# Half-array products of the mixers stage written in pairs, and retention taken two heads at a time

## The chip, the cores and the metric

The kernel runs on one core of one Trainium2 chip. The metric is the time of one execution on the device in microseconds; the figure for the kernel before is the median of its runs. TensorE multiplies matrices into PSUM, VectorE (DVE) and ScalarE (ACT) empty PSUM and do the elementwise work, GpSimd (POOL) does some elementwise work out of SBUF, and SyncE (SP) issues the loads of weights.

## The reference, cut to what matters

A first block (dilated attention, stick-breaking attention, two mixtures of experts) is followed by two layers of a second block, on 256 tokens of width 1024. A layer is `x + 0.5 ffn1`, then the mixers, then `+ 0.5 ffn2`. The mixers take `h = rmsnorm(x)`, project it with `w_in`, and run four mixers of width 256 beside each other, each with four heads of 64:

- a short convolution;
- RWKV-7 in both directions: per step `S = S * w + (S @ -kk) (kk * a)^T + v k^T`, `y = S @ r`;
- retention: `o[i] = sum_j (q_i . k_j) * gamma^|i-j| * v_j` for every head, then an RMS norm and a SiLU gate;
- MLA, an attention with low-rank queries and keys.

Their outputs, side by side, go through `w_out` and are added to `x`.

## The kernel before, in words

Everything is fp32. The large projections are split into three fp32r products each (`mm3`, L243 to L247); the small products inside the mixers are plain fp32 (`mm`, L249 and L250), and the trace shows two matmul records for each of those.

`mixers` (L1105) runs once a layer. A tile keeps the features of two heads in its 128 partitions, 64 each. A product that contracts over the 64 features of one head therefore reads partitions 0 to 63 or 64 to 127, and uses the lower or the upper half of the rows of TensorE's array.

RWKV is computed in two chunks of 128 tokens (*stages*) by a chain of small products:

- **NT** (L1501 to L1509): for each group g (0, 1) and each half i (0, 1), four products of 64 x 128 by 128 columns (two directions d, two head pairs hp) into one PSUM buffer psC, and one masked multiply of 128 x 512 on VectorE that empties it into NT.
- **the M chain** (L1532 to L1605): the inverse of each head's triangular matrix, first in squares of 32 rows, with a VectorE step after each set of products, two groups in turn, then the larger blocks with F, H and X.
- **products(stage, d, hp)** (L1514 to L1525): for each half hh one psC buffer, a product of KA with 256 columns and one of BE with 128 columns, and one masked multiply of 128 x 384 on VectorE. It is called four times for stage 0 before the stages (L1611) and once in each of the last four steps of stage 0 for stage 1 (L1661), there behind the copy of a psC buffer to ysum.
- the steps R, U, S and ysum of both stages.

In the trace AR, an input of NT and of `products`, appears as tile x.

The rest of the stage is a generator, `pieces` (L1310): the rotary products, retention, the latents of MLA, the convolution, MLA's attention and the first parts of the output projection, cut into pieces by `yield`. `fill()` (L1487) lets the generator go on by as many pieces as the next digit of `TURNS` (L163) says; it stands behind each step of the chain, so that TensorE has projections and other work while VectorE and ScalarE finish a link.

**Retention** in `pieces`: `head(h)` (L1338) makes two score products (64 rows, 256 columns, keys j = 0, 1, each into a psB buffer), each emptied by a multiply with the decay on VectorE (L1345), then four value products into a third psB buffer, and an eviction into yr (rT in the trace). Heads 0 and 1 are called at the second and the fourth step of the gate's projection (L1357 to L1360), head 2 behind the first latent (L1367), head 3 behind the other latents (L1380).

PSUM: psA has four buffers (projections), psB two, psC two. `evac` (L533) empties PSUM by ScalarE and VectorE in turn. Tiles of one name share their buffers in rotation; a new one waits for the release of the oldest. "t", which holds the scores, has eight. The framework sets each engine's order when it builds the program: among the instructions whose inputs and buffers are ready by its plan, the earliest in the code goes first, and later work may go ahead of earlier work that waits.

Of the kernel before, what the change touches and what calls it, by code (L numbers as in the profile page):

```python
# [11 lines left out]
OP = mybir.AluOpType  # L12
# [157 lines left out]
class Net:  # L170
# [934 lines left out]
    def mixers(self, x, l):  # L1105
        nc, A = self.nc, self.A
        v, act, gp = nc.vector, nc.scalar.activation, nc.gpsimd
        tt, stt, ts = v.tensor_tensor, v.scalar_tensor_tensor, v.tensor_scalar
        with self.tc.tile_pool(name="mix", bufs=1) as sp:
# [4 lines left out]
            def new(name, n=256, dt=F32):  # L1114
                return sp.tile([128, n] if isinstance(n, int) else n, dt, name=name, bufs=bufs.get(name, 1))
# [55 lines left out]
            chs = lambda c: slice(c * 128, c * 128 + 128)  # L1171
# [15 lines left out]
            AR, KA, BE, fac, wa, E = {}, {}, {}, {}, {}, {}  # L1187
# [3 lines left out]
            for h in range(2):  # L1191
                w4 = self.row().rearrange("p (d a t) -> p d a t", d=2, a=2)
                LL = self.row()[:, :516].rearrange("p (d c t) -> p d c t", d=2, c=2)
                for d in range(2):
                    wa[d, h] = w4[:, d]
                    r = slice(64 * d, 64 * d + 64)
                    p = self.psC()
# [8 lines left out]
                    for c in range(2):  # L1206
                        o, i = raw[:, c, inc(d)], wa[d, h][:, 0, chs(c)]
                        if d:
                            o, i = o[:, ::-1], i[:, ::-1]
# [14 lines left out]
            for h in range(2):  # L1224
                p = chunk(2 + h)
# [26 lines left out]
            for h in range(2):  # L1252
                p = self.psC()
# [3 lines left out]
            for d, h in both:  # L1257
                t = new("t")
# [21 lines left out]
            u, out = {}, {}  # L1280
# [29 lines left out]
            def pieces():  # L1310
                p = yield from chunk_parts(21)
# [4 lines left out]
                qk = {}  # L1316
                for n, i in (("q", 7), ("k", 9)):
                    for hp in range(2):
                        q = new("t")
                        p = yield from chunk_parts(i + hp)  # L1320
                        self.evac(q, p[:, :256])
                        p = self.psB()
                        self.mm(p[:, :256], self.r64, q)
                        o, t = new("rq"), new("t")
# [10 lines left out]
                rv, rg, yr = new("kT", [128, 2, 256]), new("kf", [128, 2, 256]), new("rT", [128, 8, 64])  # L1335
                yield from rows(1, lambda c, p: self.evac(rv[:, c, :], p))

                def head(h):  # L1338
                    r = slice(h % 2 * 64, h % 2 * 64 + 64)
                    ST = []  # L1340
                    for j in range(2):
                        p = self.psB()
                        self.mm(p[:, :256], qk["k", h // 2][r, chs(j)], qk["q", h // 2][r, :])
                        st = new("t")
                        tt(out=st, in0=p[:, :256], in1=self.decay[:, h, 128 * (1 - j):128 * (1 - j) + 256], op=OP.mult)  # L1345
                        ST.append(st)
                    p = self.psB()
                    for c in range(2):
                        for j in range(2):
                            self.mm(p[:, c * 64:c * 64 + 64], ST[j][:, chs(c)], rv[:, j, h * 64:h * 64 + 64], j == 0, j == 1)  # L1350
                    self.evac(yr.rearrange("p (c h) d -> p c h d", c=2)[:, :, h, :], p[:, :128].rearrange("p (c d) -> p c d", c=2))

                def silu2(c, p):
                    act(rg[:, c, :], p, AF.Tanh, scale=0.5)
                    stt(out=rg[:, c, :], in0=rg[:, c, :], scalar=1.0, in1=p, op0=OP.add, op1=OP.mult)

                for h, _ in enumerate(rows(2, silu2)):  # L1357
                    if h % 2:
                        head(h // 2)
                    yield  # L1360

                late = new("late", 1664)
# [1 line left out]
                qb = late[:, :1152].rearrange("p (k c) -> p k c", k=3)  # L1364
                kvb = late[:, 1152:]
                (ckv,), rk = yield from latent((11,), 3, "la")
                head(2)  # L1367
                yield
                qa, rq = yield from latent((12, 13, 14), 0, "la")
                ex = new("t")  # L1370
# [1 line left out]
                p = self.psB()  # L1372
# [4 lines left out]
                rqs = new("rqs", 4)  # L1377
                ts(rqs[:, :2], rq, scale, None, op0=OP.mult)
                ts(rqs[:, 2:], rq, -scale, None, op0=OP.mult)
                head(3)  # L1380

                sq = g8(new("kT", [128, 2, 256]))
                act(sq, yr, AF.Square)
# [7 lines left out]
                for i, n in enumerate(("x", "c", "b")):  # L1391
                    for h in range(2):
                        p = yield from chunk_parts(15 + 2 * i + h)
# [3 lines left out]
                        elif n == "c":  # L1397
                            t = new("t", 258)
# [12 lines left out]
                for c in range(2):  # L1411
                    p = self.psB()
# [4 lines left out]
                for j in range(2):  # L1417
                    p = self.psB()
# [6 lines left out]
                for j in range(2):  # L1425
                    p = self.psB()
# [4 lines left out]
                p = self.psB()  # L1431
                for i in range(3):
                    self.mm(p[:, :256], qb[:, i, 256:], qa[i], i == 0, i == 2)
                q = new("t")
# [19 lines left out]
                for h in range(6):  # L1454
                    if h < 4:
                        p = halves(self.psB())
# [9 lines left out]
                    if 1 <= h <= 4:  # L1466
                        i, Q, m = last
                        t, pt = self.psB(), new("X", 512)
# [4 lines left out]
                        for k in range(4):  # L1473
                            self.mm(o[:, k // 2 * 64:k // 2 * 64 + 64], pt[:, chs(k)], mv[:, k % 2, i * 64:i * 64 + 64], k % 2 == 0, k % 2 == 1)
                        tt(out=ym[:, :, i * 64:i * 64 + 64], in0=o[:, :128].rearrange("p (c d) -> p c d", c=2),
                           in1=m[:, 6:8, None].to_broadcast([128, 2, 64]), op=OP.mult)
# [22 lines left out]
            fill()  # L1499
            two = range(2)  # L1500
            for g in two:  # L1501
                for i in two:
                    p = self.psC()
                    for d in two:
                        c = chunk_of(g, d)
                        for hp in two:
                            x0, x1 = AR[d, hp][half(i), c, 0, :], BE[d, hp][half(i), chs(c)]
                            self.mm(p[:, chs(2 * d + hp)], *((x0, x1) if d else (x1, x0)))
                    tt(out=NT[:, 8 * g + i:8 * g + 8:2, :], in0=p.rearrange("p (q t) -> p q t", q=4), in1=self.nmask, op=OP.mult)  # L1509
            fill()  # L1510

# [2 lines left out]
            def products(stage, d, hp):  # L1514

                c = chunk_of(stage, d)
                t = self.row().rearrange("p (h a t) -> p h a t", h=2, a=4)
                for hh in two:
                    ar = AR[d, hp][half(hh), c, :, :]
                    p = self.psC()  # L1520
                    self.mm(p[:, :256], KA[d, hp][half(hh), chs(c)], ar)
                    self.mm(p[:, 256:384], BE[d, hp][half(hh), chs(c)], ar[:, 1, :])
                    tt(out=t[:, hh:hh + 1, :3, :], in0=p[:, :384].rearrange("p (h a t) -> p h a t", h=1, a=3),
                       in1=self.gmask[d], op=OP.mult)
                G[stage, d, hp] = t  # L1525
# [218 lines left out]
```

## Time and profile before

| | us |
|---|---|
| median of 3 runs | 2017.63 |
| lowest, highest run | 2016.68, 2024.1 |
| the profiled execution, its own time | 2027.7 |
| its span | 2025.7 |
| TensorE busy | 1919.8 (95%) |
| VectorE busy | 1186.3 (59%) |
| ScalarE busy | 862.8 (43%) |
| GpSimd busy | 193.3 (10%) |

The span runs from the first to the last instruction; the execution's own time has some 2 us around it. TensorE counts as busy while a matmul is under way, and matmuls overlap, so the time that a group costs is read from its first start to the start of what follows it, not from the length of its records. The mixers of layer 0 lie at about 1039 to 1206 us of the span, those of layer 1 at 1643 to 1815 us.

### The profile page before, as it was taken

To read this page: it belongs to the slowest core of one execution; us is meant where nothing else is said; L and a number is where in the kernel's file an instruction comes from. 1 tells how busy PE (TensorE), PEld (TensorE's weight loads), DVE (VectorE), ACT (ScalarE), POOL (GpSimd) and SP (SyncE) were. 2 spreads that over 40 slices of the span, in tenths; PEclk is the share of its full clock that TensorE was granted. 3 is DMA by queue.
4 is the path that set the end of the run, shared out by engine and by line. 5 is a ranking of instruction groups with operands and counts; after the bars stand their busy time and mean duration, and the time that the engine had idled before them with its cause. 6 is when DMAs were issued, how large, how long until landed. Compare 5 with 4: busy or idle time off the path is not lost. (4 is left out here: it accounts for less than half of the span.)

```text
span 2025.7 us, 36997 instructions
## 1 busy us (share of the span) xinstructions
PE 1919.8 (95%) x14866; PEld 1622.0 (80%) x14866; DVE 1186.3 (59%) x2329; ACT 862.8 (43%) x1786; POOL 193.3 (10%) x225
## 2 busy tenths in 40 slices
PE   7999997997897997999999999999999999999998
PEld 7999996434885443899888988998999888888997
DVE  6778775125876124855576556555555675556554
ACT  5656552112662112544543335445544533235443
POOL 1323220000220000000021100000000030100000
PEclk9999998998998998999998999999999999899999
DMA  8345346795436796655532215555555532215553
GB/s 280 126 137 164 127 135 240 278 408 191 146 125 222 268 388 232 211 188 187 184 113 77 93 62 178 185 188 168 199 187 188 188 103 83 84 61 176 189 186 107
DMA packets 102516, 357.10 MB, mean 176 GB/s; under 512 B 11888, under 2 KB 15136, under 8 KB 102208
## 3 DMA queue, kind: packets, MB, share of 16 engines
q1 hardware_dynamic: 97584, 341.70, 49.1%
q10 hardware_dynamic: 4704, 12.81, 2.0%
q8 instruction: 120, 1.97, 0.4%
q14 instruction: 60, 0.49, 0.1%
q0 software_dynamic: 48, 0.13, 0.0%
HBM read 353.53 MB, written 1.07 MB: 175 GB/s over the span
## 5 line engine op out<-in xcount | busy, mean ns | idle before, releaser
L241 DVE TENSOR_TENSOR wlo<-raw,whi 128x512 fp32r<-128x512 f32 (+1 forms) x910 | 626.1, 715 | 384.0 <-ACT whi L240 380.1
L240 ACT ACTIVATE whi<-raw 128x512 fp32r<-128x512 f32 (+1 forms) x910 | 529.8, 616 | 592.3 <-issue 197.6
L245 PE MATMUL psB<-xTh,whi 128*128 128x256 f32 x1792 | 507.7, 283 | 12.3 <-ACT whi L240 8.3
L247 PE MATMUL psB<-xTh,wlo 128*128 128x256 f32 x1792 | 506.4, 283 | 0.2 <-DVE wlo L241 0.2
L246 PE MATMUL psB<-xTl,whi 128*128 128x256 f32 x1792 | 506.1, 282 | 0.4
L245 PEld LDWEIGHTS psB<-xTh,whi 128*128 128x128 f32 x1792 | 340.1, 190 | 18.1 <-ACT whi L240 9.8
L246 PEld LDWEIGHTS psB<-xTl,whi 128*128 128x128 f32 x1792 | 340.1, 190 | 5.4 <-DVE xTl L241 1.5
L247 PEld LDWEIGHTS psB<-xTh,wlo 128*128 128x128 f32 x1792 | 340.3, 190 | 1.4 <-DVE wlo L241 0.7
L247 PE MATMUL psA<-whi,hl 128*128 128x512 f32 x352 | 139.5, 396 | 0.0
L245 PE MATMUL psA<-whi,hh 128*128 128x512 f32 x352 | 139.4, 398 | 0.0
L246 PE MATMUL psA<-wlo,hh 128*128 128x512 f32 x352 | 138.7, 394 | 0.0
L245 PE MATMUL psA<-xTh,whi 128*128 128x256 f32 (+1 forms) x352 | 107.8, 307 | 0.3 <-ACT vt L536 0.2
L247 PE MATMUL psA<-xTh,wlo 128*128 128x256 f32 (+1 forms) x352 | 105.1, 299 | 0.0
L246 PE MATMUL psA<-xTl,whi 128*128 128x256 f32 (+1 forms) x352 | 103.6, 295 | 0.3 <-DVE xTl L241 0.3
L245 PE MATMUL psB<-whi,xTh 128*128 128x384 f32 (+2 forms) x256 | 90.3, 353 | 3.6 <-DVE qs L547 1.7
L247 PE MATMUL psB<-whi,xTl 128*128 128x384 f32 (+2 forms) x256 | 88.7, 347 | 0.4 <-DVE xTl L241 0.3
L246 PE MATMUL psB<-wlo,xTh 128*128 128x384 f32 (+2 forms) x256 | 88.5, 346 | 0.3 <-DVE wlo L241 0.3
L296 POOL TENSOR_TENSOR ss<-ss,mh 128x1 f32<-128x1 f32 x14 | 9.8, 702 | 785.5 <-DVE ss L295 780.8
L250 PE MATMUL psB<-raw,XT 128*64 128x512 f32 x288 | 83.5, 601 | 0.0
L247 PEld LDWEIGHTS psA<-whi,hl 128*128 128x128 f32 x352 | 66.0, 188 | 16.8 <-DVE hl L241 0.7
L246 PEld LDWEIGHTS psA<-wlo,hh 128*128 128x128 f32 x352 | 66.6, 189 | 12.6
L245 PEld LDWEIGHTS psA<-whi,hh 128*128 128x128 f32 x352 | 66.3, 188 | 12.8 <-ACT hh L240 0.9
(414 smaller groups left out, 3036.1 us busy)
## 6 DMA issues: line engine op xcount, KB each, us to landing
raw<-in_ffn1gu_dram SPq DMA_DIRECT2D x88, 512.0 KB, 3.8
raw<-in_ffn2gu_dram SPq DMA_DIRECT2D x88, 512.0 KB, 3.7
raw<-in_egu_dram SPq DMA_DIRECT2D x72, 512.0 KB, 9.9
wf<-in_egu_dram SPq DMA_DIRECT2D x56, 512.0 KB, 8.6
raw<-in_dqk_dram SPq DMA_DIRECT2D x46, 512.0 KB, 3.9
raw<-in_ffn1dn_dram SPq DMA_DIRECT2D x44, 512.0 KB, 3.6
raw<-in_ffn2dn_dram SPq DMA_DIRECT2D x44, 512.0 KB, 3.6
raw<-in_wb_dram SPq DMA_DIRECT2D x40, 512.0 KB, 3.7
```

The costliest lines, as they stand in the source:

```text
L240: self.hi = self.nc.scalar.activation(hi, src, AF.Copy)
L241: return (self.nc.gpsimd if pool else self.nc.vector).tensor_tensor(out=lo, in0=src, in1=hi.bitcast(F32), op=OP.subtract)
L245: mm(out, a[0], b[0], start=start, stop=False)
L246: mm(out, a[0], b[1], start=False, stop=False)
L247: mm(out, a[1], b[0], start=False, stop=stop)
L250: return self.nc.tensor.matmul(out, a, b, start=start, stop=stop)
L296: nc.gpsimd.tensor_tensor(out=ss[:, 3:4], in0=ss[:, 2:3], in1=self.mh[:, :1], op=OP.pow)
```

## The change

Three places in `mixers`:

- NT: both psC buffers of a group are taken first, and the products of the two halves alternate; then both buffers are emptied.
- `products`: both psC buffers are taken first, then KA of both halves, BE of both halves, and both multiplies.
- Retention: `heads(hp)` takes two heads. For each j it takes two psB buffers, makes the score of both heads (one on each half of the rows), and empties both; the eight value products of both heads go into one psB buffer, emptied by one eviction. `heads(0)` stands where head 0 stood, `heads(1)` where head 2 stood; the calls for heads 1 and 3 are gone from their places.

The numbers of products and of multiplies stay as they are; `TURNS` is not changed.

```diff
--- before.py
+++ after.py
@@ -1335,28 +1335,32 @@
                 rv, rg, yr = new("kT", [128, 2, 256]), new("kf", [128, 2, 256]), new("rT", [128, 8, 64])
                 yield from rows(1, lambda c, p: self.evac(rv[:, c, :], p))
 
-                def head(h):
-                    r = slice(h % 2 * 64, h % 2 * 64 + 64)
-                    ST = []
+                def heads(hp):
+
+                    ST = {}
                     for j in range(2):
-                        p = self.psB()
-                        self.mm(p[:, :256], qk["k", h // 2][r, chs(j)], qk["q", h // 2][r, :])
-                        st = new("t")
-                        tt(out=st, in0=p[:, :256], in1=self.decay[:, h, 128 * (1 - j):128 * (1 - j) + 256], op=OP.mult)
-                        ST.append(st)
-                    p = self.psB()
-                    for c in range(2):
-                        for j in range(2):
-                            self.mm(p[:, c * 64:c * 64 + 64], ST[j][:, chs(c)], rv[:, j, h * 64:h * 64 + 64], j == 0, j == 1)
-                    self.evac(yr.rearrange("p (c h) d -> p c h d", c=2)[:, :, h, :], p[:, :128].rearrange("p (c d) -> p c d", c=2))
+                        ps = [self.psB() for _ in range(2)]
+                        for i in range(2):
+                            r = slice(i * 64, i * 64 + 64)
+                            self.mm(ps[i][:, :256], qk["k", hp][r, chs(j)], qk["q", hp][r, :])
+                        for i, p in enumerate(ps):
+                            st = ST[i, j] = new("t")
+                            tt(out=st, in0=p[:, :256], in1=self.decay[:, 2 * hp + i, 128 * (1 - j):128 * (1 - j) + 256], op=OP.mult)
+                    p = self.psB()[:, :256].rearrange("p (c h d) -> p c h d", c=2, h=2)
+                    for i in range(2):
+                        h = 2 * hp + i
+                        for c in range(2):
+                            for j in range(2):
+                                self.mm(p[:, c, i, :], ST[i, j][:, chs(c)], rv[:, j, h * 64:h * 64 + 64], j == 0, j == 1)
+                    self.evac(yr.rearrange("p (c h) d -> p c h d", c=2)[:, :, 2 * hp:2 * hp + 2, :], p)
 
                 def silu2(c, p):
                     act(rg[:, c, :], p, AF.Tanh, scale=0.5)
                     stt(out=rg[:, c, :], in0=rg[:, c, :], scalar=1.0, in1=p, op0=OP.add, op1=OP.mult)
 
                 for h, _ in enumerate(rows(2, silu2)):
-                    if h % 2:
-                        head(h // 2)
+                    if h == 1:
+                        heads(0)
                     yield
 
                 late = new("late", 1664)
@@ -1364,7 +1368,7 @@
                 qb = late[:, :1152].rearrange("p (k c) -> p k c", k=3)
                 kvb = late[:, 1152:]
                 (ckv,), rk = yield from latent((11,), 3, "la")
-                head(2)
+                heads(1)
                 yield
                 qa, rq = yield from latent((12, 13, 14), 0, "la")
                 ex = new("t")
@@ -1377,7 +1381,6 @@
                 rqs = new("rqs", 4)
                 ts(rqs[:, :2], rq, scale, None, op0=OP.mult)
                 ts(rqs[:, 2:], rq, -scale, None, op0=OP.mult)
-                head(3)
 
                 sq = g8(new("kT", [128, 2, 256]))
                 act(sq, yr, AF.Square)
@@ -1499,13 +1502,14 @@
             fill()
             two = range(2)
             for g in two:
-                for i in two:
-                    p = self.psC()
-                    for d in two:
-                        c = chunk_of(g, d)
-                        for hp in two:
+                ps = [self.psC() for _ in two]
+                for d in two:
+                    c = chunk_of(g, d)
+                    for hp in two:
+                        for i in two:
                             x0, x1 = AR[d, hp][half(i), c, 0, :], BE[d, hp][half(i), chs(c)]
-                            self.mm(p[:, chs(2 * d + hp)], *((x0, x1) if d else (x1, x0)))
+                            self.mm(ps[i][:, chs(2 * d + hp)], *((x0, x1) if d else (x1, x0)))
+                for i, p in enumerate(ps):
                     tt(out=NT[:, 8 * g + i:8 * g + 8:2, :], in0=p.rearrange("p (q t) -> p q t", q=4), in1=self.nmask, op=OP.mult)
             fill()
 
@@ -1515,11 +1519,12 @@
 
                 c = chunk_of(stage, d)
                 t = self.row().rearrange("p (h a t) -> p h a t", h=2, a=4)
+                ps = [self.psC() for _ in two]
                 for hh in two:
-                    ar = AR[d, hp][half(hh), c, :, :]
-                    p = self.psC()
-                    self.mm(p[:, :256], KA[d, hp][half(hh), chs(c)], ar)
-                    self.mm(p[:, 256:384], BE[d, hp][half(hh), chs(c)], ar[:, 1, :])
+                    self.mm(ps[hh][:, :256], KA[d, hp][half(hh), chs(c)], AR[d, hp][half(hh), c, :, :])
+                for hh in two:
+                    self.mm(ps[hh][:, 256:384], BE[d, hp][half(hh), chs(c)], AR[d, hp][half(hh), c, 1, :])
+                for hh, p in enumerate(ps):
                     tt(out=t[:, hh:hh + 1, :3, :], in0=p[:, :384].rearrange("p (h a t) -> p h a t", h=1, a=3),
                        in1=self.gmask[d], op=OP.mult)
                 G[stage, d, hp] = t
```

## Rows read from the trace of the kernel before

**Rows 1.** Busy us by stretch: length, PE, PEld, DVE, ACT, POOL, clock, DMA
```profile
1039.00:1206.00 167.00, 163.85 (x2317) 144.22 (x2317) 99.06 (x233) 50.90 (x120) 20.22 (x30) 0.94 0.27 87
1643.00:1815.00 172.00, 167.13 (x2320) 146.68 (x2321) 100.41 (x234) 51.17 (x121) 20.22 (x30) 0.92 0.26 84
1102.28:1115.93 13.65, 13.65 (x148) 12.96 (x148) 5.53 (x13) 3.14 (x9) 0.00 (x0) 0.50 0.23 80
1692.78:1699.61 6.83, 6.83 (x164) 6.36 (x165) 2.31 (x6) 1.15 (x2) 0.00 (x0) 0.50 0.02 5
1726.90:1740.57 13.67, 13.67 (x63) 11.42 (x62) 4.39 (x12) 2.44 (x5) 2.49 (x6) 0.50 0.12 40
```

**Rows 2.** TensorE in order of time (start, length): one piece, layers 0 and 1
```profile
1102.39 0.69 PE L250 MATMUL psB<-kT,t 128*128 128x64 f32 x2
...
1116.20 0.50 PE L250 MATMUL psC<-H,NT 64*64 64x64 f32 x5
...
1710.48 0.43 PE L250 MATMUL psB<-kT,t 128*128 128x64 f32 x2
...
1718.41 0.56 PE L250 MATMUL psC<-H,NT 64*64 64x64 f32 x6
```

**Rows 3.** Groups of matmuls, both mixers (count | busy us, mean ns | idle)
```profile
L250 PE MATMUL psC<-x,KA 64*128 64x256 f32 x64 | 16.9, 446 | 0.0
...
L250 PE MATMUL psB<-rq 64*128 64x256 f32 x32 | 10.5, 443 | 0.0
```

**Rows 4.** TensorE in order of time: a stage-0 products piece and what follows
```profile
1130.98 0.71 PE L250 MATMUL psC<-x,KA 64*128 64x256 f32 x4
1131.52 0.39 PE L250 MATMUL psC<-x,BE 64*128 64x128 f32 x4
1131.84 0.38 PE L245 MATMUL psA<-xTh,whi 128*128 128x256 f32 x1
```

**Rows 5.** In order of time: stage-1 products (TensorE), and the copy to ysum (VectorE)
```profile
1172.43 0.93 PE L250 MATMUL psC<-x,KA 64*128 64x256 f32 x3
...
1190.60 0.70 PE L250 MATMUL psC<-x,KA 64*128 64x256 f32 x2
1191.14 0.38 PE L250 MATMUL psC<-x,BE 64*128 64x128 f32 x2
1191.45 0.33 PE L1470 MATMUL psB<-c0t,w 128*128 128x128 f32 x1
...
1172.53 0.29 DVE L538 COPY ysum<-psC 128x128 f32<-128x128 f32 x1
```

**Rows 6.** TensorE in order of time: NT products of layer 0
```profile
1047.24 0.56 PE L250 MATMUL psC<-BE,x 64*128 64x128 f32 x1
1047.25 0.56 PE L250 MATMUL psC<-x,BE 64*128 64x128 f32 x1
...
1049.06 0.50 PE L250 MATMUL psC<-x,BE 64*128 64x128 f32 x3
1049.40 0.61 PE L250 MATMUL psC<-BE,x 64*128 64x128 f32 x4
```

**Rows 7.** VectorE by line: NT's evictions, the decay multiplies (ns min/median/max)
```profile
L1509 DVE TENSOR_TENSOR NT<-psC,c2t x8: 669/680/692, 1048.0 to 1655.9; 128x512 f32<-128x512 f32 x8
...
L1345 DVE TENSOR_TENSOR t<-psB,c2t x16: 413/420/425, 1085.4 to 1730.8; 128x256 f32<-128x256 f32 x16
```

**Rows 8.** TensorE in order of time: retention's scores, and a wait behind them
```profile
1084.43 1.13 PE L250 MATMUL psB<-rq 64*128 64x256 f32 x4
1085.49 0.45 PE L250 MATMUL psC<-M,NT 32*32 32x32 f32 x30
...
1094.45 0.43 PE L250 MATMUL psB<-kT,t 128*128 128x64 f32 x2 [0.47 <-DVE t L1345]
...
1100.20 0.70 PE L250 MATMUL psB<-rq 64*128 64x256 f32 x2
1100.83 0.31 PE L250 MATMUL psC<-M,NT 32*32 32x32 f32 x8
```

## The prediction, made before the changed kernel was run

> **What bounds the kernel now.** I read the busy time by stretch first, since the change lies in the mixers stage alone, which runs twice, once a layer. In both runs of it TensorE is busy 97 to 98% of the stretch, VectorE 58 to 59% and ScalarE 30% [rows 1]. So TensorE is the bound here, and a change is worth what it takes off TensorE's own queue, as long as other matmuls are there to move up. The same view shows the second bound: in three stretches, 34.15 us together, TensorE was granted 0.50 of its clock, which is 1.2 GHz of its 2.4 [rows 1]. What that costs is read from the same piece of the program at either level: from the third head's value products to the first product on H it is 13.81 us in layer 0, nearly all of it in the slow stretch, and 7.93 us in layer 1 at full clock [rows 2]. 13.65 us of half clock thus cost 5.9 us, 0.43 us for each.
>
> Then I read the groups of matmuls for how much the change touches: 64 records of KA products and 32 of retention's scores, all on 64 rows [rows 3]. Every fp32 product leaves two records, so these are 32 and 16 products in both layers; NT's are 16 a layer by the code. Last I read them in order of time, to see which of them already run in twos.
>
> **Already in twos: the stage-0 products.** The code issues KA and BE of one half and then KA and BE of the other. The rows have all four records of KA ahead of all four of BE: the piece takes 0.54 us for KA and 0.32 us for BE [rows 4]. Where one half runs by itself, in stage 1, its two records of KA take 0.54 us and its two of BE 0.31 us [rows 5]. Two halves cost what one costs: both ran at once without being written next to each other, the second half overtaking the first half's BE. The eight stage-0 pieces (four a layer) look alike, so there the new order saves nothing.
>
> The Trainium skill ("TensorE: Matmul & The Clock Gate", Part 3, what overlaps and what doesn't) says that matmuls start and end strictly in program order. By that rule the old order could overlap only the first half's BE with the second half's KA, and the change would save in these pieces too; the rows above speak against it (rival E).
>
> **The stage-1 products** are not in twos: 0.85 us for each half [rows 5], against 0.86 us for both [rows 4]. The bound above is 0.84 us for each of the eight pieces, 6.7 us. But what parts them is not the order of the code. A piece starts when one of the two psC buffers is free; the other still holds the output, whose copy to ysum (0.29 us) runs only after KA of the first half has begun [rows 5], and other ready work slips in, like the transposes at 1191.45. The change asks for both buffers first, but the copy still ends when it ends. I take 0. The bound below is that KA of the second half now waits in the queue ahead of the first half's BE, which then starts after it: 0.31 us eight times, 2.5 us lost.
>
> **The NT products.** Three records of one half in a row take 0.34 us, 0.112 us each, so a product costs 0.22 us; where the halves meet, at 1047.24, two records start 0.01 us apart [rows 6]. Of a layer's 16 products two pairs do that already (the other at the start of group 1), so they stand in 14 slots; fully paired they would stand in 8. The bound above is 6 x 0.224 = 1.34 us a layer, 2.7 us in all. Against it stands the eviction: one multiply of 0.68 us for each buffer on VectorE [rows 7], two buffers, and the change fills both before it empties either. For group 1 the first buffer comes free 0.68 us before the second; the order on each engine takes what is ready, so the first half's four products go first, as now. In group 0 all inputs come at once but for the last pair, and two slots go: 0.45 us a layer. I take 0.9 us for both layers. Bound below: nothing gained, and both evictions uncovered, 1.36 us a layer, 2.7 us. What covers them now is projections of the next pieces; I cost the wait at nothing, since group 0's end and group 1 lie between two turns of fill.
>
> **Retention.** Two scores of one head, on the same rows, take 1.06 us and one takes 0.63 us [rows 8]: 0.43 us a product, and 0.20 us for coming from and going to another shape. A new piece of two heads has two pairs. The first finds both psB buffers free and saves one product, 0.43 us. The second pair needs the buffers that the first pair's multiplies empty, 0.42 us each, one after the other [rows 7], so its second product may start 0.42 us late, which is the length of the first: between 0 and 0.43 us, and I take half, 0.21 us, since TensorE at 98% busy often comes late. That makes 0.64 us a piece, and there are four pieces: 2.6 us. The bounds are 0.86 us a piece, 3.4 us in all, and below, no gain and two multiplies uncovered, 0.84 us a piece, 3.4 us lost. Waiting products hold up all of TensorE's queue, the M chain included; now this happens once for 0.47 us [rows 8].
>
> The number of decay multiplies stays at 16 in all [rows 7], that of value products too; four evictions become two in each layer. Both hide under TensorE, and I cost them at nothing; without that cover it would be a gain of the two evictions. No DMA is added or moved. ScalarE and VectorE take turns at evictions, so those between the old second and fourth head swap engines: nothing, both engines have idle time [rows 1]. Head 1's work leaves the fill after the second gate projection and head 3's the one after the latents. The work that covered the chain there is less by 1.06 us of scores and their value products; the projections of these turns are left as cover, and later ready work moves up.
>
> **Sum.** 2.6 + 0.9 + 0 + 0 = 3.5 us less. The profiled execution took 2027.7 us, of which 2025.7 us are its span; so it would take 2024.2 us. The median of the runs shown is 2017.63 us, 10 us below that execution, which is in the size of its slow-clock stretches (34.15 x 0.43 = 14.7 us). Taken off the median: 2014.1 us. All bounds above together are 3.4 + 2.7 + 6.7 = 12.8 us less, 2004.8 us; all bounds below are 3.4 + 2.7 + 2.5 = 8.6 us more, 2026.2 us.
>
> **The rivals.** A measurement of this kernel can tell some 0.5%, 10.1 us, from no change: below 2007.5 us is faster, above 2027.7 us slower.
>
> B: the evictions set the pace. Both buffers full, VectorE empties them one by one, and TensorE waits for the second; what pairing gives in a group, 0.45 to 1.34 us a layer for NT, is less than or like the 1.36 us of two evictions [rows 7]. For it: group 1 and the second pair of scores must wait. Against it: other matmuls fill such waits now. Time: 2017.6 us. The Trainium skill ("TensorEngine Tiling (Array Packing)", "PSUM Bottleneck") says that packing speeds up TensorE but not the emptying of PSUM, which may then be the limit; its advice to use both engines for that is not taken here, since the masks' multiplies are all on VectorE.
>
> C: faster through the clock. The stretch at 1102.28 begins right behind half-array scores and 32-row squares [rows 8]; layer 0 fell at 1102.28 and layer 1, same program, did not at that place [rows 1, 2]. So it is a near thing, and denser scores may tip it. If half of the 34.15 us goes, that is 7.3 us on top of 3.5: 2006.8 us. If they go entirely, 1999.4 us.
>
> D: slower through the clock. Place: the stretch from the latents to the stage-0 products, which loses the fourth head, and the fill after the second gate projection, which loses the second. With less for TensorE to do between the links of the chain the clock falls there in a layer where it did not. Price: one more stretch of 13.65 us in each layer, 11.8 us, less 3.5: 2025.9 us. It decides from 3.5 / 0.43 = 8.1 us of additional half clock on.
>
> E: matmuls keep the order of issue and only neighbours overlap, so the stage-0 pieces gain too: a piece would take 0.43 + 0.43 + 0.22 + 0.20 = 1.28 us now and 0.86 us then, 3.4 us over eight pieces, giving 2010.7 us. The rows [rows 4] already show 0.86.
>
> **How the numbers follow.** The forecast gets 0.42, B 0.20, C 0.20, D 0.15 and E 0.03. Faster by over 0.5% needs most of C (0.14) or the stage-1 pieces paired as well (0.06 of the forecast): 0.20. Slower by over 0.5% needs D with uncovered waits on top (0.09) or B with all bounds below (0.03): 0.12. The rest, 0.68, lies between. The range is that of the bounds, 2004 to 2026 us: it holds the forecast, B, E and most of D, and leaves out the far ends of C and D, some 0.15. Within 0.5% the forecast's own range is 2009 to 2018 us.
>
> **What would show it.** Right: the scores of a piece as two pairs whose records start some 0.01 us apart, a piece's first pair taking about 0.63 us; the stage-0 pieces still at 0.86 us; stage 1 with KA of the second half still waiting for the copy; four slots fewer of NT in both layers. Wrong: TensorE idle before the second pair or before NT's group 1 with VectorE's multiply as what ended it (B); a total of half clock in the mixers that differs by more than 8 us from 34.15 (C, D); stage-1 pieces near 0.86 us (more gain than forecast).

## The result and the profile after

The changed kernel took 2032.74 us (median of 9 runs, 2025.11 to 2040.78), the kernel before 2018.38 us beside it (9 runs, 2010.14 to 2024.1). The ratio is 1.0059, with a 95% interval of 1.0037 to 1.0082: about 12 us slower. (Ratios here and below are estimated from all runs with their interval; they are not the quotient of the medians, which lie 14.4 us apart here.) The prediction, 2014.1 us with a range up to 2026 us and a chance of 0.12 for this side, was wrong. The profiled execution took 2034.94 us, 2033.2 of them span.

First the windows again, of the profile after (stretch, length, busy time and instructions of PE, PEld, DVE, ACT and POOL, granted clock, DMA share and GB/s). The first two lines are the mixers of both layers, as in [rows 1]. The next two are the part of them that the change moved things in, from the first retention score to the product that leaves the gate. The last two are the longest stretches at half clock in them.

```profile
1042.00:1211.00 169.00, 164.04 (x2303) 143.40 (x2304) 95.58 (x226) 49.51 (x117) 19.26 (x30) 0.92 0.26 86
1650.00:1821.00 171.00, 165.89 (x2312) 144.88 (x2313) 97.06 (x230) 49.90 (x118) 19.26 (x30) 0.92 0.26 85
...
1088.80:1211.10 122.30, 119.76 (x1189) 105.82 (x1189) 66.33 (x165) 40.37 (x99) 11.39 (x20) 0.92 0.23 76
1696.50:1818.90 122.40, 119.91 (x1190) 105.96 (x1189) 66.32 (x165) 40.37 (x99) 11.37 (x20) 0.92 0.23 76
1105.23:1125.71 20.48, 20.48 (x181) 17.44 (x181) 7.57 (x20) 6.14 (x16) 0.72 (x1) 0.50 0.16 56
1712.80:1733.20 20.40, 20.40 (x180) 17.35 (x181) 7.71 (x20) 6.29 (x16) 0.72 (x1) 0.50 0.16 56
```

The part from the first score to the gate in the kernel before, same view:

```profile
1084.40:1203.00 118.60, 117.61 (x1189) 104.72 (x1189) 67.39 (x166) 40.76 (x100) 11.81 (x20) 0.94 0.24 78
1689.40:1811.20 121.80, 120.08 (x1190) 106.51 (x1189) 67.77 (x166) 40.64 (x100) 11.83 (x20) 0.92 0.23 75
```

The same number of matmuls takes 3.7 and 0.6 us longer. TensorE's idle time in it (length less busy time) grew from 1.0 and 1.7 us to 2.5 us in each layer. In this part each layer now has one fall of the clock to 0.50 (1.2 GHz) that lasts 20.4 us, and both begin at the same place of the program. Before, the two layers fell at different places, once for 13.65 us and once for 6.83 and 13.67 us [rows 1]. The execution profiled of before was itself one of the slower ones (2027.7 us against a median of 2018.38), so the clock is better compared over all runs: the mean granted clock of a run has its median at 0.968 in the 9 runs after, and at 0.974 in the 94 runs of before that were taken beside the experiments. A mean lower by 0.006 is 0.012 of the span more at half clock, 24 us; at 0.43 us each [rows 2] that makes 10.4 of the 12 us. The clock of a run is known to 0.001, which is 1.7 us, so this is an estimate. Another comes from the 94 runs of before alone: in a straight line through them, 0.001 less of the mean clock goes with 1.48 us more. By that line the clocks of the nine runs after (mean 0.968, against 0.973 before) explain 7.4 us, and the runs lie another 4.4 us above it. So the clock is some 7 to 10 of the 12 us.

TensorE in order of time where the fall begins, layer 0 after (start, length, engine, line, operation, count, and in brackets the idle time before it with what ended it):

```profile
1101.59 0.28 PE L247 MATMUL psA<-xTh,wlo 128*128 128x256 f32 x1
1101.80 0.69 PE L250 MATMUL psC<-M,NT 32*32 32x32 f32 x32
1103.15 0.50 PE L250 MATMUL psC<-M,NT 32*32 32x32 f32 x18 [0.65 <-DVE M L1559]
1104.69 0.61 PE L250 MATMUL psB<-c0t,t 128*128 128x1 f32 x4 [1.05 <-ACT t L1287]
1105.23 1.22 PE L250 MATMUL psB<-rq 64*128 64x256 f32 x2
```

VectorE, and under it ScalarE, at the same time:

```profile
1101.01 1.75 DVE L241 TENSOR_TENSOR wlo<-raw,whi 128x512 fp32r<-128x512 f32 x2 [0.57 <-ACT whi L240]
1102.68 0.41 DVE L1559 TENSOR_TENSOR M<-M,psC 128x256 f32<-128x256 f32 x1
...
1103.61 0.63 ACT L1576 ACTIVATE F<-Mt 32x128 f32<-32x128 f32 x2 [2.11 <-DVE Mt L1560]
1104.26 0.38 ACT L1287 ACTIVATE t<-psA 128x256 f32<-128x256 f32 x1
```

This is the fill after the second gate projection, without head 1. TensorE ran out of projections at 1101.8. Both waits come out of one link of the chain. The addition to M needs the squares that end at 1102.49; it starts 0.19 us later, behind two weight splits on VectorE, and takes 0.41 us, and with no projection left to do meanwhile TensorE waits 0.65 us for it. ScalarE sat idle for 2.11 us until Mt was there, and only behind two copies of it takes the square (L1287) of the latent that TensorE has projected. The sums over that square wait 1.05 us, and the next heads' scores, which don't need them, stand behind the sums in TensorE's queue. In the kernel before, TensorE has one wait in this stretch (1084 to 1130; what was waited for: us in total, times, longest), and it is not at this place [rows 8]:

```profile
PE psB L250 <- DVE t L1345: 0.5, 1, 0.5
```

In the changed kernel the clock falls at 1105.2, with the first scores after the second wait: they take 1.22 us for two records (0.70 us for two at full clock [rows 8]).

What the change was meant to do, it did where buffers were free. The scores of heads 0 and 1, after:

```profile
1088.83 0.70 PE L250 MATMUL psB<-rq 64*128 64x256 f32 x4
1089.46 0.50 PE L250 MATMUL psC<-M,NT 32*32 32x32 f32 x30
1090.22 1.03 PE L250 MATMUL psB<-rq 64*128 64x256 f32 x4 [0.26 <-DVE t L1348]
1091.18 0.31 PE L250 MATMUL psC<-M,NT 32*32 32x32 f32 x12
```

The first pair takes 0.63 us from its start to the next piece, as one product did [rows 8]. The second waits 0.26 us for the multiply and takes 0.96 us, since its second product waits again: 1.22 us in all, where two scores in a row took 1.06 [rows 8].

The products after: the first piece of stage 0, the fourth one, and the last piece of stage 1.

```profile
1138.20 0.70 PE L250 MATMUL psC<-x,KA 64*128 64x256 f32 x4
1138.74 0.39 PE L250 MATMUL psC<-x,BE 64*128 64x128 f32 x4
1139.06 0.39 PE L245 MATMUL psA<-xTh,whi 128*128 128x256 f32 x1
...
1148.42 0.70 PE L250 MATMUL psC<-x,KA 64*128 64x256 f32 x2
1148.95 0.38 PE L250 MATMUL psC<-x,BE 64*128 64x128 f32 x2
1149.26 0.70 PE L250 MATMUL psC<-x,KA 64*128 64x256 f32 x2
1149.80 0.38 PE L250 MATMUL psC<-x,BE 64*128 64x128 f32 x2
1150.11 0.38 PE L245 MATMUL psA<-xTh,whi 128*128 128x256 f32 x1
...
1198.72 0.70 PE L250 MATMUL psC<-x,KA 64*128 64x256 f32 x2
1199.25 0.38 PE L250 MATMUL psC<-x,BE 64*128 64x128 f32 x2
1199.56 0.33 PE L1473 MATMUL psB<-c0t,w 128*128 128x128 f32 x1
```

The first three pieces of stage 0 in a layer still take 0.54 + 0.32 us [rows 4]. The fourth does not: its halves go one behind the other, 1.69 us in both layers, where before it took 0.86 us. The fourth piece before, and under it the last of VectorE's multiplies ahead of the fourth piece, before and after:

```profile
1141.29 0.71 PE L250 MATMUL psC<-x,KA 64*128 64x256 f32 x4
1141.82 0.40 PE L250 MATMUL psC<-x,BE 64*128 64x128 f32 x4
1142.15 0.38 PE L245 MATMUL psA<-xTh,whi 128*128 128x256 f32 x1
...
1140.57 0.55 DVE L1523 TENSOR_TENSOR row<-psC,c2t 128x384 f32<-128x384 f32 x1
...
1148.65 0.55 DVE L1528 TENSOR_TENSOR row<-psC,c2t 128x384 f32<-128x384 f32 x1
```

Before, that multiply had emptied the second psC buffer (1141.12) when the piece began at 1141.29. After, the piece begins at 1148.42 in the first buffer, and KA of the second half starts 0.06 us behind the multiply's end at 1149.20. In stage 1 one half still takes 0.53 + 0.31 us by itself [rows 5], and all its pieces keep their lengths to 0.01 us. NT's products, the end of group 0 and then group 1:

```profile
1050.40 0.67 PE L250 MATMUL psC<-x,BE 64*128 64x128 f32 x3
1050.80 0.37 PE L250 MATMUL psC<-BE,x 64*128 64x128 f32 x1
1050.90 0.27 PE L250 MATMUL psC<-x,BE 64*128 64x128 f32 x1
1051.01 0.39 PE L250 MATMUL psC<-BE,x 64*128 64x128 f32 x3
...
1052.96 0.71 PE L250 MATMUL psC<-x,BE 64*128 64x128 f32 x4
1053.51 0.61 PE L250 MATMUL psC<-BE,x 64*128 64x128 f32 x4
1054.05 0.39 PE L245 MATMUL psA<-xTh,whi 128*128 128x256 f32 x1
1054.37 0.71 PE L250 MATMUL psC<-x,BE 64*128 64x128 f32 x4
```

In group 1 the halves still go one behind the other, with projections between them. In group 0 few records start together. Counted one by one, the 32 records of a layer had four such twos before (starts within 0.03 us), which makes two pairs of products; after there are two of them, one pair of products, in both layers. NT is in pairs less often than it was.

### The profile page after: what moved, and what is told of

Same layout as the page of the kernel before. It is cut to its first block, busy times and chain, and to the rows that moved or that the text cites. A ratio compares the mean times of both kernels' runs of the same rounds, so it can differ in the third digit from the quotient of the medians.

```text
span 2033.2 us, 36991 instructions
## 1 busy us (share of the span) xinstructions
PE 1923.7 (95%) x14866; PEld 1622.1 (80%) x14866; DVE 1182.4 (58%) x2327; ACT 862.8 (42%) x1784; POOL 192.2 (9%) x225
```

## The experiments

The theory: the loss comes from the places. With head 1 gone from the gate's fourth turn, the fill there no longer covers the chain of M and of the latent, and the clock falls. The rivals: the paired scores wait for their multiplies; the new order of the products or of NT costs time; or the other place, behind the latents, is the one that matters.

**The three parts alone** (each one of the three hunks of the diff, the other two as before).

> NT's products in pairs alone, retention and the stage products as before. Places theory (the loss comes from the new places of retention's heads: TensorE idles where the second head was, and the clock falls): within 3 us of before; from the second score product on the stage runs as before. Buffers theory (both PSUM buffers filled before either is emptied costs the time): 3 to 6 us slower, with TensorE idle ahead of group 1 and VectorE's NT multiply as what ended it.

> The stage products in pairs alone. Places theory: no difference (within 2 us), a stage-0 piece at 0.86 us as before and a stage-1 half at 0.85 us. Buffers theory: 2 to 3 us slower, since KA of the second half waits for the copy to ysum ahead of BE of the first.

> Retention by two heads alone, NT and stage products as before. Places theory: 8 to 14 us slower, all of the change's loss, with the idle ahead of the latent's sum (about 1.05 us, ended by ScalarE L1287) and three quanta of half clock behind it, 20.5 us, in both layers. Buffers theory: 3 to 6 us slower, and the rest in e1 and e2.

Measured against before (2018.4 us, 30 runs): NT 2018.08 us, 0.9993 (0.9971 to 1.0014); products 2020.21 us, 1.0008 (0.9986 to 1.0031); retention 2031.3 us, 1.0056 (1.0038 to 1.0075). Retention alone has the whole loss. Its half clock is not what was expected (20.5 us in both layers): it is 17.1 us in layer 0, and 6.8 us in layer 1, there ahead of the latent's sums and not behind them.

**The places without the pairs**: single heads, as before, where the change put them.

```diff
-                    if h % 2:
-                        head(h // 2)
+                    if h == 1:
+                        head(0)
+                        head(1)
...
                 head(2)
+                head(3)
...
-                head(3)
```

> Heads as before, one after the other with their own buffers, but at the places of the change: heads 0 and 1 at the second step of the gate's projection, heads 2 and 3 behind the first latent. Places theory: 8 to 14 us slower, like e3, with the same idle and the same half clock, though nothing is paired. Buffers theory: within 3 us of before, since no piece fills both buffers for two heads at once.

Measured: 2039.81 us (7 runs), 1.0077 (1.0045 to 1.0109). Without one pair of scores the loss is all there, so the pairs' waits are not its cause.

**One place at a time**: the first hunk of that diff alone, then the other two alone.

> Only head 1 moved: single heads 0 and 1 both at the second step of the gate's projection, heads 2 and 3 where they were. If the loss comes from the fill after the gate's fourth step (where head 1 was), this alone is 8 to 14 us slower, with the idle of 1 us ahead of the latent's sum and half clock behind it in both layers. If it comes from the end of the latents (where head 3 was), it is within 3 us of before.

> Only head 3 moved: single heads 2 and 3 both behind the first latent, heads 0 and 1 where they were. If the loss comes from the fill where head 1 was: within 4 us of before. If it comes from the place of head 3, or from the two heads crowded behind the first latent: 8 to 14 us slower.

Measured against before (2019.33 us, 29 runs): head 1 moved, 2032.32 us (6 runs), 1.0063 (1.004 to 1.0086); head 3 moved, 2023.78 us, 1.0011 (0.9987 to 1.0035). TensorE's waits from 1084 to 1130 with head 1 moved (what was waited for: us in total, times, longest):

```profile
PE psB L250 <- ACT t L1287: 1.1, 1, 1.1
PE psC L250 <- DVE M L1555: 0.7, 1, 0.7
```

The windows from the first score to the gate in the same kernel, layers 0 and 1:

```profile
1087.80:1209.40 121.60, 119.37 (x1189) 105.56 (x1189) 67.62 (x166) 40.60 (x100) 11.86 (x20) 0.93 0.23 77
1695.10:1816.80 121.70, 119.47 (x1190) 105.63 (x1189) 67.62 (x166) 40.72 (x100) 11.87 (x20) 0.93 0.23 76
```

These are the two waits of the changed kernel, with no pair in the program, and the clock falls at the same place, for 17.1 us in either layer. It is the fill after the second gate projection.

**More work in that place**: retention by two heads, and head 1 computed once more, by itself, where it stood before. It writes the same values again, and all else is as in the retention experiment.

```diff
                     if h == 1:
                         heads(0)
+                    if h == 3:
+                        head(1)
                     yield
```

> Retention by two heads as in e3, and head 1 computed once more, as a single head, at the gate's fourth step, with the same values written again: 2 us of TensorE work more in each layer, for nothing but fill. Idle and clock theory: although it does 4 us more work than e3, it is faster than e3 by 3 to 12 us, without the idle of 1 us ahead of the latent's sum and with less than 10 us of half clock between the scores and the latents. If the work on TensorE alone set the time: 3 to 5 us slower than e3, 2035 us.

Measured: 2017.02 us, 0.9986 (0.9972 to 1.0001), 14 us under the retention experiment's median, with more to compute. TensorE's waits from 1084 to 1130:

```profile
PE psB L250 <- DVE t L1364: 0.5, 1, 0.5
PE psB L250 <- DVE t L1348: 0.3, 1, 0.3
```

The windows from the first score to the gate:

```profile
1085.30:1199.20 113.90, 112.34 (x1201) 99.43 (x1201) 68.57 (x167) 40.44 (x100) 11.85 (x20) 1.00 0.25 81
1682.60:1795.90 113.30, 111.91 (x1201) 99.07 (x1201) 66.72 (x167) 40.80 (x100) 11.30 (x20) 1.00 0.24 81
```

The waits for M and for the square are gone, and the clock is 1.00 through both stretches. The twelve more records in each layer are the repeated head.

**Half of that work**: the same, but of head 1 only the two scores and their multiplies, whose results nobody uses.

> Retention by two heads as in e3, and at the gate's fourth step only the two score products and multiplies of head 1 once more, unused: about half of the fill of e7, 1.1 us of TensorE instead of 2. If the clock falls by a tipping point and this is enough: 2015 to 2022 us. If the loss follows the length of the idle: about half of e3's loss, 2024 us. If it is too little to tip: as e3, 2031 us.

Measured against before (2022.24 us, 35 runs): 2027.84 us, 1.0021 (0.9994 to 1.0049), some half of the retention experiment's loss by its middle; the interval holds no loss at all as well as most of it. In the profile the wait for M is gone and that for the square is not (waits from 1084 to 1130):

```profile
PE psB L250 <- ACT t L1287: 1.0, 1, 1.0
```

Both layers of that execution fell for 20.5 us.

**Pairs, and the fill kept**: the scores of two heads as in the change, but the value products of each pair stand where head 1 and head 3 stood.

```diff
+                    return ST
+
+                def values(hp, ST):
                     p = self.psB()[:, :256].rearrange("p (c h d) -> p c h d", c=2, h=2)
...
-                        heads(0)
+                        ST = heads(0)
+                    if h == 3:
+                        values(0, ST)
...
-                heads(1)
+                ST = heads(1)
...
                 ts(rqs[:, 2:], rq, -scale, None, op0=OP.mult)
+                values(1, ST)
```

> Retention by two heads with the scores paired as in e3, but the value products of heads 0 and 1 moved to the gate's fourth step and those of heads 2 and 3 behind the other latents, where heads 1 and 3 were: the same work as e3, spread over the old places. Idle and clock theory: the pairs' gain of 1 to 2 us a layer stays and the fill is back, so 0 to 5 us faster than before, and 10 to 18 us faster than e3. If pairing itself cost the time: as slow as e3.

Measured: 2014.44 us, 0.9975 (0.9962 to 0.9989): faster than the kernel before. TensorE's waits from 1084 to 1130:

```profile
PE psC L250 <- issue: 1.6, 1, 1.6
PE psB L250 <- ACT t L1287: 0.3, 1, 0.3
```

The windows from the first score to the gate:

```profile
1089.80:1203.10 113.30, 110.78 (x1190) 98.36 (x1189) 66.85 (x165) 40.54 (x99) 11.98 (x20) 0.98 0.25 81
1689.60:1802.80 113.20, 110.95 (x1189) 98.50 (x1189) 66.84 (x165) 40.54 (x99) 11.96 (x20) 0.98 0.25 81
```

The wait at the latent's sums is 0.3 us, and the clock doesn't fall there. It falls at the other wait, of 1.6 us behind the first scores ("issue": the engine waited for nothing that the profile shows), and comes back within 3.4 us.

**The split on top of the rest**: the whole change with only the first pair's values moved back; with both moved back; and with both moved back, NT in pairs and the products as before.

> The whole change, with one thing put back: the value products of heads 0 and 1 stand at the gate's fourth step, where head 1 was; heads 2 and 3 stay together behind the first latent as in the change. Fill theory (the loss hangs on the fill at that one place): within 4 us of before, 2014 to 2022 us, with at most 7 us of half clock a layer between the scores and the end of the mixers. If the crowding behind the first latent or the pairs elsewhere cost as much: above 2026 us.

> The whole change, with the value products at the old places of heads 1 and 3, for both pairs. Fill theory: e8 gave 0.25% with retention alone; NT gave nothing and the stage products cost 1 us a layer or nothing, so 2 to 6 us faster than before, 2012 to 2017 us. If the three parts of the change hinder each other: slower than before.

> NT in pairs and retention split as in e8, the stage products as before. Fill theory: 4 to 7 us faster than before, at or 1 to 2 us below e10 (the stage products' new order taken out). If the new order of the stage products is worth something after all: 1 to 3 us slower than e10.

Measured against before (2022.24 us, 35 runs), in this order: 2021.05 us, 1.0002 (0.9978 to 1.0026); 2019.94 us, 0.9989 (0.9963 to 1.0014); 2016.58 us, 0.998 (0.996 to 1.0). Moving one piece of value products back takes the changed kernel from 1.0059 to no loss. The clock of the first of the three missed its expectation, though, with 13.7 us of half clock in layer 0. The two kernels that split the values and leave the products as before (0.998, and 0.9975 above) have the lowest ratios of all, but the intervals overlap with that of the split with the new products.

**The stretches side by side.** Half-clock time is the sum of the stretches at 0.50 in it; from a window's clock it comes out as (1 - clock) x 2 x length, but for rounding. The third column takes off 0.43 us for each us of it [rows 2]: an estimate of what the program would take at full clock. The last is TensorE's idle time right before the first of the latent's sums, with a star where the clock fell there (from 0.3 us before the sums to 3.0 us behind them). Layer 0 / layer 1, one execution each.

```
kernel                  length         half clock    length at full clock   idle at the sums
before                  118.6 / 121.8  13.7 / 20.5   112.7 / 113.0          0    * / 0
the change              122.3 / 122.4  20.5 / 20.5   113.5 / 113.5          1.05 * / 1.05 *
NT alone                112.7 / 112.6   0   /  0     112.7 / 112.6          0      / 0
products alone          113.6 / 117.6   0   /  6.8   113.6 / 114.7          0      / 0
retention alone         119.7 / 115.9  17.1 /  6.8   112.4 / 113.0          1.05 * / 0.99
places, no pairs        121.6 / 120.8  17.1 / 13.7   114.3 / 115.0          1.05 * / 1.05 *
head 1 moved            121.6 / 121.7  17.1 / 17.1   114.3 / 114.3          1.05 * / 1.05 *
head 3 moved            112.5 / 121.2   0   / 17.1   112.5 / 113.9          0      / 0    *
head 1 repeated         113.9 / 113.3   0   /  0     113.9 / 113.3          0      / 0
half of it              121.7 / 121.8  20.5 / 20.5   112.9 / 113.0          1.03 * / 1.04 *
pairs, values split     113.2 / 113.2   3.4 /  3.4   111.8 / 111.7          0.31   / 0.18
whole, first pair split 117.4 / 114.4  13.7 /  3.4   111.5 / 112.9          0.28 * / 0
whole, values split     117.4 / 121.3  13.7 / 20.5   111.5 / 112.5          0.15 * / 0    *
NT and pairs, split     110.7 / 116.4   0   / 13.7   110.7 / 110.5          0.30   / 0.30 *
```

In these executions the change would be within 1 us of before in either layer at full clock. A fall is not certain: one and the same program can have 0 in one layer and 13.7 in the other, and the runs of before alone spread over 25 us. But with idle time at the sums it is likelier here. Of the ten layers with some 1 us of it nine fell there, for 13.7 to 20.5 us; of the eighteen with 0.31 us or less six did, for 13.7 to 17.1 us. Over the runs this is the lower mean clock.

## Why the prediction was wrong, step by step

**The step that failed** is the one on the places: "The work that covered the chain there is less by 1.06 us of scores and their value products; the projections of these turns are left as cover, and later ready work moves up", costed at nothing. The projections left ran out at 1101.8, and nothing moved up, since the order of TensorE's queue is set when the program is built: the next heads' scores stood behind the waiting sums. Moving head 1 alone costs as much as the whole change (1.0063 against 1.0059), and putting it back as a repeat takes the loss away; half of it takes away about half by its middle, which its interval doesn't settle. The direct price is the smaller one, 0.65 + 1.05 us of idle time in layer 0 and 0.55 + 1.05 in layer 1. The larger one is the clock, an estimated 7 to 10 us.

**Rival D** named this fill and this mechanism, and had a chance of 0.15. Its price of 11.8 us for the clock was somewhat high, against the 7 to 10 us above. What it set against that, the 3.5 us of the sum, wasn't there; in its place stood the uncovered waits of 3.3 us in both layers and 1.7 us of the products (below). That 2017.63 + 11.8 is 2029.4 us, and the ratio of 1.0059 puts the change at 2029.5 us on the same base, is therefore luck in part: too much for the clock and nothing for the rest. "Needs D with uncovered waits on top" fits what was found, but 0.09 was too low a chance for it. D should have been the forecast: the trace had shown that the clock fell there in one layer of two [rows 1], and the change took 1.06 us of scores and four products out of just that fill. Its other place, where head 3 was, gave nothing that could be measured (1.0011). The total of 34.15 us that the prediction took for the half clock of the mixers left out two stretches: the windows' own clocks of 0.94 and 0.92 make 47.6 us [rows 1]. The profile after has 54.4 us by the same sum, 7 us more and not the 8 that were to show D: one execution of each doesn't show what the clocks of all runs show.

**Retention, 2.6 us**, was right for the first pair and too much for the second. The first took the 0.63 us that I gave it. For the second I had taken a gain of 0.21 us; with its wait it took 1.22 us against 1.06, a loss of 0.16 [rows 8]. With the fill kept, the stretches at full clock are 0.9 and 1.3 us shorter than before, 2.2 us together, and by the ratio the kernel is 5.0 us faster (2.2 to 7.7 by the interval). That is near 2.6, but in a kernel with other places, so it doesn't confirm the sum. At the changed places the pairs win some 2 us a layer (114.3 and 115.0 against 112.4 and 113.0), and the places had cost about that much.

**NT, 0.9 us**, was wrong in its sign. Group 0 did not gain its two slots and has one pair, as before; group 1 stayed unpaired, as forecast, but lost even the one pair at its start. That is a slot more in each layer, some 0.2 us. 0.9993 can't tell this from nothing. Rival B, the evictions as the pace, would show as waits for NT's multiply on VectorE, and TensorE's waits have none; for the scores it does show, with 0.26 us once a layer.

**Stage 0, nothing**, failed for one piece of four: 0.86 us in either order for the other three, but 1.69 us for the fourth, 0.83 us lost in each layer, 1.7 us in all. All four kernels that were run with the new order lose some 0.8 us a layer there, and none of the others does. The forecast asked whether the old pieces could gain; it did not ask whether the new order would still find both buffers free. For the others rival E is out. The Trainium skill's rule of strict program order ("TensorE: Matmul & The Clock Gate", Part 3) would have had the new order save time in these pieces; no row here shows it.

**Stage 1, 0 with 2.5 us lost as the bound below**, was right: its pieces keep their lengths. The 0.85 us for each half were read from the last piece of a layer alone; the first takes 1.30 us in both kernels, since its halves overlap in part. By the table the products alone are 0.9 and 1.7 us longer at full clock, and the whole change with split values is 0.8 and 2.0 us longer than the same without the products. Stage 0's pieces account for 0.8 us of each: in the whole change with split values the fourth takes 1.68 us, and with the products alone the third and the fourth together take 2.55 us instead of 1.79. What makes layer 1 longer still isn't traced. By the runs the products alone are no different from before (1.0008, an interval of 0.9986 to 1.0031).

**Rival C**, that denser scores hold the clock up, isn't seen: the mean clock with pairs and the fill kept is 0.975, against 0.974.

**What stays open.** That the fill at this place decides, the runs show. How the clock decides is not settled: falls at the latent's sums come with idle time of 1.05 us, but six of eighteen layers without it fell there as well, among them layer 0 of before, at 1102.28, where the wait next to that in its rows is 0.47 us, at 1094.45 [rows 8]. A kernel that keeps the idle time and holds the clock wasn't tried, so the division into 7 to 10 us of clock and the rest is estimated from profiles and mean clocks, not made on the chip. `TURNS` was left as it was; whether other pieces of the generator could have filled the place wasn't tried either.

## What to carry to other kernels

A piece of independent work that stands between the links of a dependent chain has two prices: its own time, and the time of the gap that it fills; joining two such pieces to save a part of the first price can cost more than it saves. Cost the place that a moved piece leaves: what TensorE has left there, and which wait stands at the head of its queue. Where pieces are to be joined, take together only what the array does at once (here the scores), and leave the rest (here the value products) as fill where it was. A pair needs both of its buffers free at once; look at what empties them, since a piece that gets them one by one runs half by half, as the fourth piece of stage 0 and NT's group 1 did.

## What was not expected of the hardware

- More work in the right place made the program faster: 12 records a layer more, and 14 us less than without them.
- What a fall of the clock costs went with where it began: behind 1.1 to 1.7 us of idle time near the first scores it lasted 3.4 or 6.8 us, at the latent's sums 13.7 to 20.5 us, with TensorE busy in all of the 20.48 us at 0.50 in the profile after.
- In the changed kernel the clock fell at the sums with no gap over 1.05 us on TensorE since the first score, and in six layers of other kernels with 0.31 us or less right before the sums.
- Two products on different halves of the rows run at once even where one stands behind another product of the first half in the code: KA, BE, KA, BE and KA, KA, BE, BE both take 0.54 + 0.32 us when both buffers are free. The counter steps in the trace's records agree with queues in the code's orders (before, BE of either half adds more than one to TensorE's semaphore; after, the first more than one, the second one), so the overtaking is the engine's.
